# Delta rule on one Trainium2 core: wider spacing of the inverse's stages, later transposes, and the first block's low weight parts in four pieces

## The chip, the cores and the metric

The kernel runs on one core of a Trainium2 chip. The metric is the device time of one execution in microseconds. Before the change three runs gave 2961.45, 2965.48 and 2971.93 us, with a median of 2965.48 us.

## What is computed

A decoder of two layers over 2048 tokens of width 1024, in float32. The first layer is a gated delta rule with 8 heads of 128, the second a forgetting attention. The change lies in the first layer alone, which is, cut to what matters:

```python
def chunk_gated_delta_rule(q, k, v, g, beta):
    ...
    a_mat = jnp.where(strict, jnp.einsum('bhncd,bhnsd->bhncs', kb, kc) * decay, 0.0)
    sol = lax.linalg.triangular_solve(a_mat, rhs, left_side=True, lower=True, unit_diagonal=True)
    u, w = sol[..., :Dv], sol[..., Dv:]
    ...
    # for each chunk in turn
    v_new = u_i - w_i @ S
    o = (q_i * exp(g_i)) @ S + attn_i @ v_new
    S = S * exp(g_last) + k_dec.T @ v_new

def gdn_mixer(h, w_in, ...):
    qkv, z, a, b = split(h @ w_in)
    qkv = silu(causal_depthwise_conv(qkv, conv_w))   # 4 taps
    ...
    o = rms_norm(o, o_norm) * silu(z)
    return o @ w_out
```

## The kernel before

**Projections.** `gdn` works on four blocks of 512 tokens and in each on four groups of two heads. `project` (L272) computes for a group eight products of 1024 x 128 weights with the block: for each head k, q and v, and then z of both. A product has eight steps. A step is `mm3` (L129): three matmuls of 512 columns, since each operand is kept as a high part that TensorE's fast float32 format holds (wh, xh) and the low rest (wl, xl). A group has thus 64 steps, numbered 1 to 64 here.

**Weights.** In the first block (qt 0) `wsplit` (L283) loads a weight, and `split` (L122) makes the high part by a ScalarE copy (L124) and the low part by one GpSimd subtraction of 1024 columns (L125). Both are stored to `w_d` and loaded from there in the other three blocks (L289, L290). In a group there are eight weights, in the first block 32.

**Tails.** After a product of k, q or v its `tail` (L340) makes the convolution: two ScalarE passes (L343, L347), three VectorE multiply-adds (L349), a tanh on ScalarE (L352) and a last VectorE step into `kq` or `th` (L357). What it returns, `rest` (L361), is kept in `pend` and called in the product after next, behind the step kt == 3: four TensorE transposes (L364), squares (L368), kd (L371) or vR (L398) on ScalarE, and for q the norms (a power on GpSimd, L119), the k k^T products (L387) and the matrix At on VectorE (L391). So k, q, v of the first head and k, q, v of the second have their transposes in steps 20, 28, 36, 44, 52 and 60.

**The inverse and the chain.** `finish` (L416) is a generator that works on a group behind its projections. It sends At through DRAM (L426, L429), inverts 32 x 32 blocks by 31 rounds of a multiply and a subtraction on VectorE (L435, L437), sends the result back (L440, L442), transposes blocks of it into Tn (L445), and joins the blocks by two pairs of TensorE products: px (L451) and py (L462, L464), with a copy X1 between them (L455 on ScalarE, L456 on VectorE), then px2 (L475) and py2 (L482). Then come four chunks with the state S in three stages each (A, B, C: L497, L515, L523), and the outputs: two transposes pto (L554), each followed by a product og on VectorE (L556) and a store (L558). px, py, px2, py2, the chunks and pto take turns in two PSUM banks (pool `gcs`, tag `sc`).

**What sets the order.** `weave` (L587) runs a step of the projections and then looks at each open `finish`: a stage that yields W is followed by W main steps, and the next stage is written behind the step after these. With the weights before, px stands at step 44 of the following group, py at 48, px2 at 51, py2 at 53, the first A at 56, and the two pto at steps 31 and 33 of the group after that. The last group's `finish` runs beside the output projection `Wout.run` (L648, 256 such steps); the next part of the kernel (`hprep`, L732) is begun after it. The written order is what a scheduler starts from: it fixes the order on each engine and on each DMA queue from readiness and this priority, so that an instruction can stand earlier than it is written. Each engine then works in its fixed order, and so does the SP queue, which issues all DMAs here.

Of the kernel before, what the change touches and what calls it, by code (L numbers as in the profile page):

```python
# [14 lines left out]
ALU = mybir.AluOpType  # L15
# [7 lines left out]
KT = D // P  # L23
# [14 lines left out]
def f(ap):  # L38
    return ap.bitcast(F32)
# [82 lines left out]
def split(k, hi, lo, src, eng=None):  # L122

    i = k.nc.scalar.copy(hi, src)  # L124
    (eng or k.nc.vector).tensor_tensor(out=lo, in0=src, in1=f(hi), op=ALU.subtract)  # L125
    return i.ins


def mm3(nc, out, ah, al, bh, bl, start, stop):  # L129
    nc.tensor.matmul(out, ah, bh, start=start, stop=False)  # L130
    nc.tensor.matmul(out, ah, bl, start=False, stop=False)  # L131
    nc.tensor.matmul(out, al, bh, start=False, stop=stop)  # L132


def gdn(k, ins, oT_d, chain, proj_, after_proj):

    nc, tc = k.nc, k.tc
# [55 lines left out]
    def keep():  # L193
        ct, wh, wl = kept.pop(0)
        nc.sync.dma_start(w_d[ct, 0], f(wh))
        nc.sync.dma_start(w_d[ct, 1], f(wl))
# [75 lines left out]
    def project(qt, hg, state, tiles):  # L272
# [10 lines left out]
        def wsplit(col, nm):  # L283

            ct = col // P
            wh = p2.tile([P, KT, P], F32R, tag="wh", bufs=4, name=f"wh_{nm}")
            wl = p2.tile([P, KT, P], F32R, tag="wl", bufs=4, name=f"wl_{nm}")
            if qt > 0:
                nc.sync.dma_start(f(wh), w_d[ct, 0])  # L289
                nc.sync.dma_start(f(wl), w_d[ct, 1])  # L290
                return wh, wl
            wr = p2.tile([P, D], F32, tag="x", bufs=4, name=f"wr_{nm}").rearrange("p (t c) -> p t c", c=P)
            nc.sync.dma_start(wr, w_in[:, col:col + P].rearrange("(t p) c -> p t c", p=P))
            split(k, wh, wl, wr, nc.gpsimd)
            kept.append((ct, wh, wl))
            if len(kept) > 2:
                keep()
            return wh, wl

        def proj(col, nm):  # L300
            wh, wl = wsplit(col, nm)
            pp = pm.tile([P, TB], F32, tag="mm", name=f"pp_{nm}")
            for kt in range(KT):
                mm3(nc, pp, wh[:, kt, :], wl[:, kt, :], xh[kt], xl[kt], kt == 0, kt == KT - 1)
                if kt == 3 and len(pend) > 1:
                    pend.pop(0)()
                yield
            return pp

        for hl in range(G):  # L310
# [11 lines left out]
            for i, gg in enumerate((gh, gl)):  # L322
                nc.gpsimd.tensor_tensor(out=rg[:, i], in0=bc(k.tri, CH),
                                        in1=f(gg[:, :, h:h + 1]).to_broadcast([P, CH, P]), op=ALU.mult)
# [10 lines left out]
            for kind in (1, 0, 2):  # L335
                ct = kind * H + h
                nm = f"{q_}_{ct}"
                pp = yield from proj(ct * P, nm)

                def tail(h=h, hl=hl, us=us, kq=kq, vR=vR, kd=kd, E=E, ssn=ssn, rn=rn, vs=vs, kind=kind, ct=ct, nm=nm, pp=pp):  # L340
# [64 lines left out]
        for hl in range(G):  # L405
            h = hg * G + hl
            pp = yield from proj(3 * D + h * P, f"{q_}_z{h}")
            if hl == 0:
                pend.append(lambda: None)
            th = p2.tile([P, TB], F32, tag="th", bufs=3, name=f"thz_{q_}_{h}")  # L410
            nc.scalar.activation(th, pp, AF.Tanh, scale=0.5)
            nc.vector.scalar_tensor_tensor(out=zT[:, hl, :], in0=th, scalar=1.0, in1=pp, op0=ALU.add, op1=ALU.mult)
# [147 lines left out]
    pend = []  # L560
# [17 lines left out]

W_INV, W_PY, W_PX2, W_PY2, W_A, W_B, W_C, W_OUT, W_OUT2 = 42, 3, 2, 1, 2, 1, 2, 9, 1


H_LAG = 3
# [665 lines left out]
```

## Time and profile before

| | |
|---|---|
| median of three runs | 2965.48 us (2961.45 to 2971.93) |
| the profiled execution's own time | 2970.9 us |
| its span, first to last instruction | 2969.2 us |
| TensorE (PE) busy | 2828.0 us, 95% |
| VectorE (DVE) busy | 1747.6 us, 59% |
| ScalarE (ACT) busy | 1338.5 us, 45% |
| GpSimd (POOL) busy | 674.2 us, 23% |
| mean granted TensorE clock | 0.979 |

The first block of the projections runs to about 300 us of the span, blocks two to four to about 1222 us, and the last group's `finish` beside the output projection to about 1345 us. The rest of the span (the output projection, the shared keys and values, the attention) isn't touched.

PE is TensorE, PEld its weight load, DVE VectorE, ACT ScalarE, POOL GpSimd, SPq the queue that issues DMAs. An idle time stands with what released the instruction after it. A clock of 1.00 is the full 2.4 GHz.

### The profile page before, as it was taken

Reading aid. Unit: us, or ns where it says so; the run is one execution under the profiler, and the core shown is the slowest. Engines: PE = TensorE matmul, PEld = TensorE weight load, DVE = VectorE, ACT = ScalarE, POOL = GpSimd, SP = SyncE. Lnnn points to the kernel's source line nnn. Section 1 sums busy time; section 2 is a strip of 40 time slices with the busy share of each in tenths; the row PEclk is TensorE's granted clock in tenths of the full one; section 3 lists DMA queues with packets and bytes.
Section 4 is the critical chain, followed back from the end, with each engine's and each line's share of the span. In section 5 each row is a group of like instructions: output and inputs, shape, how many; then the busy total and the mean of one; then the engine's idle time right before and its main releaser. Section 6 shows DMA issues by size and latency. Waiting matters only on the chain.

```text
span 2969.2 us, 50594 instructions
## 1 busy us (share of the span) xinstructions
PE 2828.0 (95%) x18406; PEld 2450.9 (83%) x18406; DVE 1747.6 (59%) x5053; ACT 1338.5 (45%) x3695; POOL 674.2 (23%) x617
## 2 busy tenths in 40 slices
PE   7889999999999999899999999999999999999998
PEld 5667778777777777777899999999997888888787
DVE  6777767777777776644333223432228888888422
ACT  4445544454445444433344323443216676776421
POOL 4433111111111111022311000111004444443222
PEclk9999999999999999989999999999999999999999
DMA  6555444444443444536322323333222333232443
GB/s 215 180 176 182 163 134 146 134 151 142 135 133 127 140 134 135 155 119 195 110 90 86 96 96 111 98 101 94 96 83 89 93 100 99 91 96 82 145 147 107
DMA packets 295504, 371.63 MB, mean 125 GB/s; under 512 B 68443, under 2 KB 216150, under 8 KB 294230
## 3 DMA queue, kind: packets, MB, share of 16 engines
q1 hardware_dynamic: 295254, 368.39, 38.6%
q8 instruction: 145, 2.38, 0.3%
q14 instruction: 105, 0.86, 0.1%
HBM read 263.40 MB, written 104.92 MB: 124 GB/s over the span
## 4 chain that ended last, share of the span: by engine, by line
PE 59%; DVE 17%; issue 7%; ACT 3%; DMA 3%; POOL 3%; SPq 0%; DVEq 0%; POOLq 0%; ACTq 0%
DVE acc_q L349 4%; PE pt L1075 4%; PE ps L132 2%; PE ppv L130 2%; PE ppq L130 2%; PE ppv L131 2%; PE ppv L132 2%; PE ppq L131 2%; PE ppq L132 2%; PE ppwf L132 2%; PE ppwf L131 2%; PE ppwf L130 2%; PE ps L130 2%; PE ps L131 2%; PE ppk L130 2%
## 5 line engine op out<-in xcount | busy, mean ns | idle before, releaser
L130 PE MATMUL pp_q<-xh_q,wh_q 128*128 128x512 f32 x768 | 330.2, 430 | 2.1 <-ACT wh_q L124 2.1
L132 PE MATMUL pp_q<-xh_q,wl_q 128*128 128x512 f32 x768 | 309.0, 402 | 1.3 <-POOL wl_q L125 1.3
L131 PE MATMUL pp_q<-xl_q,wh_q 128*128 128x512 f32 x768 | 309.9, 404 | 0.0
L349 DVE SCALAR_TENSOR_TENSOR acc_q<-cx_q,cols,acc_q 128x512 f32<-128x512 f32 x288 | 226.2, 786 | 9.5 <-ACT acc_q L347 6.3
L125 DVE TENSOR_TENSOR pl<-pt,ph 128x512 fp32r<-128x512 f32 (+1 forms) x320 | 191.8, 606 | 39.4 <-ACT ph L124 37.4
L124 ACT CAST ph<-pt 128x512 fp32r<-128x512 f32 (+1 forms) x320 | 161.6, 519 | 92.2 <-PE pt L1075 91.7
L1061 ACT ACTIVATE s<-s,nm 128x128 f32<-128x128 f32 (+15 forms) x128 | 154.2, 1205 | 71.9 <-DVE nm L1059 71.9
L132 PEld LDWEIGHTS pp_q<-xh_q,wl_q 128*128 128x128 f32 x768 | 147.9, 193 | 38.2 <-POOL wl_q L125 2.0
L1075 PE MATMUL pt<-ident,s 128*128 128x128 f32 x1088 | 173.8, 274 | 2.6 <-DVE pl L125 2.5
L130 PEld LDWEIGHTS pp_q<-xh_q,wh_q 128*128 128x128 f32 x768 | 148.8, 194 | 29.6 <-ACT wh_q L124 2.2
L131 PEld LDWEIGHTS pp_q<-xl_q,wh_q 128*128 128x128 f32 x768 | 149.1, 194 | 27.2
L352 ACT ACTIVATE th_q<-acc_q 128x512 f32<-128x512 f32 x96 | 60.7, 632 | 243.5 <-DVE acc_q L349 239.5
L1075 PEld LDWEIGHTS pt<-ident,s 128*128 128x128 f32 x1088 | 134.6, 141 | 33.2 <-DVE pl L125 3.6
L130 PE MATMUL ppk<-wh_k,hh 128*128 128x256 f32 x512 | 147.7, 288 | 2.6 <-issue 2.6
L130 PE MATMUL ppq<-wh_q,hh 128*128 128x256 f32 x512 | 146.8, 287 | 0.0
L130 PE MATMUL ppv<-wh_v,hh 128*128 128x256 f32 (+1 forms) x512 | 144.9, 283 | 0.0
L131 PE MATMUL ppk<-wl_k,hh 128*128 128x256 f32 x512 | 144.5, 282 | 0.0
L132 PE MATMUL ppk<-wh_k,hl 128*128 128x256 f32 x512 | 144.3, 282 | 0.0
L130 PE MATMUL ppz<-wh_z,hh 128*128 128x256 f32 x512 | 144.3, 282 | 0.0
L132 PE MATMUL ppv<-wh_v,hl 128*128 128x256 f32 (+1 forms) x512 | 143.9, 281 | 0.0
L131 PE MATMUL ppv<-wl_v,hh 128*128 128x256 f32 (+1 forms) x512 | 143.9, 281 | 0.0
L131 PE MATMUL ppq<-wl_q,hh 128*128 128x256 f32 x512 | 143.7, 281 | 0.0
(479 smaller groups left out, 8606.5 us busy)
## 6 DMA issues: line engine op xcount, KB each, us to landing
wh_q<-w_d SPq DMA_DIRECT2D x72, 512.0 KB, 3.6
wl_q<-w_d SPq DMA_DIRECT2D x72, 512.0 KB, 4.4
wr_q<-in_gdn_w_in_dram SPq DMA_DIRECT2D x24, 512.0 KB, 5.4
w_d<-wh_q SPq DMA_DIRECT2D x24, 512.0 KB, 5.4
w_d<-wl_q SPq DMA_DIRECT2D x24, 512.0 KB, 3.6
wh_q_z<-w_d SPq DMA_DIRECT2D x24, 512.0 KB, 3.5
wl_q_z<-w_d SPq DMA_DIRECT2D x24, 512.0 KB, 4.1
x_q<-in_x_dram SPq DMA_DIRECT2D x16, 512.0 KB, 4.0
```

The source lines that it names most:

```text
L124: i = k.nc.scalar.copy(hi, src)
L125: (eng or k.nc.vector).tensor_tensor(out=lo, in0=src, in1=f(hi), op=ALU.subtract)
L130: nc.tensor.matmul(out, ah, bh, start=start, stop=False)
L131: nc.tensor.matmul(out, ah, bl, start=False, stop=False)
L132: nc.tensor.matmul(out, al, bh, start=False, stop=stop)
L349: nc.vector.scalar_tensor_tensor(out=acc, in0=cx[:, j:j + TB], scalar=cw[j], in1=acc, op0=ALU.mult, op1=ALU.add)
L352: nc.scalar.activation(th, acc, AF.Tanh, scale=0.5)
L1061: e = nc.scalar.activation(s[:, 0:w], s[:, 0:w], AF.Exp, bias=nm, accum_out=ls[:, ii:ii + 1])
L1075: nc.tensor.transpose(out=pt[:, ii * P:(ii + 1) * P], in_=Ps[ii][:, j * P:(j + 1) * P], identity=k.ident)
```

## The change

The spacing of the stages is widened: 45 main steps in place of 42 ahead of px, 5 in place of 3 ahead of py, 4 in place of 2 ahead of px2, 2 in place of 1 ahead of py2. px then stands at step 47, py at 53, px2 at 58, py2 at 61, the first A at 64, and all later stages eight steps later than before, the two pto at steps 39 and 41. `rest` is called behind kt == 6 in place of kt == 3, so that its transposes stand at steps 23, 31, 39, 47, 55 and 63. In the first block the low part of a weight is made by four GpSimd subtractions of 256 columns; the high part is made as before.

```diff
@@ wsplit, in project
-            split(k, wh, wl, wr, nc.gpsimd)
+            nc.scalar.copy(wh, wr)
+            for i in range(0, KT, 2):
+                nc.gpsimd.tensor_tensor(out=wl[:, i:i + 2], in0=wr[:, i:i + 2], in1=f(wh[:, i:i + 2]), op=ALU.subtract)
@@ proj, in project
-                if kt == 3 and len(pend) > 1:
+                if kt == 6 and len(pend) > 1:
                     pend.pop(0)()
@@
-W_INV, W_PY, W_PX2, W_PY2, W_A, W_B, W_C, W_OUT, W_OUT2 = 42, 3, 2, 1, 2, 1, 2, 9, 1
+W_INV, W_PY, W_PX2, W_PY2, W_A, W_B, W_C, W_OUT, W_OUT2 = 45, 5, 4, 2, 2, 1, 2, 9, 1
```

## Rows read from the trace of the kernel before

**Rows 1.** Stretches: us; PE, PEld, DVE, ACT, POOL busy (x); PEclk, DMA share, GB/s.

```profile
45.00:300.00 255.00, 220.06 (x1205) 175.34 (x1203) 196.26 (x480) 120.09 (x343) 101.80 (x57) 0.95 0.58 188
300.00:1222.00 922.00, 883.03 (x5650) 717.75 (x5650) 660.30 (x2177) 420.53 (x1373) 131.73 (x112) 0.98 0.42 137
1222.00:1345.00 123.00, 110.72 (x596) 88.45 (x597) 67.59 (x191) 47.97 (x125) 26.13 (x26) 0.91 0.53 165
```

**Rows 2.** Line L364 on PE, 30 to 300 us: idle until (us, times).

```profile
  DVE kq_q L357: 11.4, 3
  DVE th_q L357: 6.5, 4
```

**Rows 3.** The same line, 300 to 1222 us.

```profile
  DVE kq_q L357: 5.6, 8
  DVE th_q L357: 4.1, 2
```

**Rows 4.** Line L451 on PE, idle until: 30:300, 300:1222, 1222:1345 in turn.

```profile
  DVE Tn L445: 4.9, 2
...
  DVE Tn L445: 10.0, 14
...
  DVE Tn L445: 4.2, 1
```

**Rows 5.** Line L462 on PE, idle until: 30:300, and then 300:1222.

```profile
  ACT X_q0g L455: 2.0, 1
...
  ACT X_q2g L455: 5.3, 4
  ACT X_q3g L455: 4.8, 3
  ACT X_q1g L455: 3.2, 2
```

**Rows 6.** PE in order of time, 817 to 836 us: start, us, what, [idle before].

```profile
817.67 0.60 PE L554 MATMUL pto_q<-ident,vR_q 128*128 128x128 f32 x4
...
826.01 0.39 PE L130 MATMUL pp_q<-xh_q,wh_q 128*128 128x512 f32 x1
...
826.71 0.40 PE L130 MATMUL pp_q<-xh_q,wh_q 128*128 128x512 f32 x1
...
829.79 0.21 PE L451 MATMUL px_q2g<-Tn,At_q2g 32*32 32x32 f32 x2 [0.43 <-DVE Tn L445]
830.63 0.69 PE L451 MATMUL px_q2g<-Tn,At_q2g 32*32 32x32 f32 x30 [0.63 <-DVE Tn L445]
...
835.91 0.24 PE L462 MATMUL py_q2g<-At_q2g,X_q2g 32*32 32x32 f32 x2 [1.60 <-ACT X_q2g L455]
```

**Rows 7.** DVE in order of time, the same group's inverse and output.

```profile
787.50 0.93 DVE L435 TENSOR_TENSOR tmp_q2g<-Ti_q2g,Ai_q2g 128x31 f32<-128x31 f32 x1
...
824.13 0.74 DVE L556 SCALAR_TENSOR_TENSOR og_q<-pto_q,hon,zT_q2g 128x512 f32<-128x512 f32 x1
```

**Rows 8.** The SP queue's issues in order of time, the same group.

```profile
779.96 1.72 SPq L429 DMA_DIRECT2D Ai_q2g<-d_q2g  x4
...
824.90 0.33 SPq L558 DMA_DIRECT2D oT_d<-og_q  x1
825.40 1.88 SPq L442 DMA_DIRECT2D At_q2g<-d_q2g  x4
```

**Rows 9.** Groups of POOL, 30 to 310 us: busy us, mean ns, idle before.

```profile
L125 POOL TENSOR_TENSOR wl_q<-wr_q,wh_q 128x1024 fp32r<-128x1024 f32 x24 | 57.5, 2397 | 111.2 <-ACT wh_q L124 80.0 <-PE pa_q0g L498 20.0 <-ACT sp_e_q L98 11.1
L119 POOL TENSOR_TENSOR rn_q<-ssn_q,mhalf 128x8 f32<-128x8 f32 x7 | 11.5, 1643 | 26.7 <-DVE ssn_q L374 20.2 <-DVE cx_q L342 4.2 <-DMA w_d<-wh_q_z 2.3
L323 POOL TENSOR_TENSOR rg_q<-tri,gl_q 128x512 fp32r<-128x512 f32 x8 | 8.9, 1108 | 0.0
```

**Rows 10.** Line L437 alone, two groups of heads: DVE busy us (x), clock, DMA.

```profile
176.00:258.00 82.00, 11.66 (x31) 0.96 0.59 187
491.00:561.00 70.00, 7.22 (x31) 1.00 0.44 142
```

## The prediction

> **What bounds the kernel now.** I read the table of stretches first. TensorE is busy in 883.03 of the 922 us of the projection blocks two to four and in 220.06 of 255 us of the first block [rows 1]: it is the engine that the stage waits for, so a wait of TensorE is time of the kernel, and time at the lower clock is too. The granted clock has two levels, 2.4 GHz (1.00) and 1.2 GHz (0.50), so (1 - mean) x length is about what the slow time costs: 255 x 0.05 = 12.8 us, 922 x 0.02 = 18.4 us, 123 x 0.09 = 11.1 us [rows 1].
>
> Then I read who ended TensorE's idle time, line by line. It stands in three places: ahead of a head's transposes L364, which wait for VectorE's last step of the tail (L357): 17.9 us in the first block, 9.7 us later [rows 2, 3]; ahead of the inverse's first product px (L451), which waits for VectorE's transposes Tn (L445): 4.9, 10.0 and 4.2 us [rows 4]; ahead of py (L462), which waits for ScalarE's copy X1 (L455): 2.0 us and 5.3 + 4.8 + 3.2 = 13.3 us [rows 5]. That is 62 us of waits, which the edits aim at one by one. Last I read one group in order of time [rows 6 to 8].
>
> One step of the main loop (three matmuls) starts 0.70 us after the one before: 826.01 to 826.71 [rows 6]. All shifts below are counted in it.
>
> **Transposes three steps later** (`kt == 6`): TensorE reaches each L364 three steps, 2.1 us, later, with the same instructions; nothing is added. In blocks two to four eight waits total 5.6 us, 0.7 us each, and go; two total 4.1 us, and as they are unequal I leave 1.0: 8.7 us gained [rows 3]. In the first block three waits total 11.4 us and four 6.5 us [rows 2]; 2.1 us from each of the long ones and the short ones whole I put at 5.5 + 4.8 = 10.3, leaving 7.6. Ends: nothing (VectorE is later by as much), and 27.6 us. What is queued behind: the head's squares, kd and vR copies on ScalarE, the power on GpSimd, At on VectorE, and the eight DMAs that carry At to the inverse (L426, L429, four each) on SP, all 2.1 us later. These are the price, and they decide the next part.
>
> **W_INV 42 to 45.** px comes at side step 47 in place of 44, 2.1 us later, but the At that feeds the inverse is 2.1 us later as well. Whether anything is gained depends on where the inverse's chain waits. Its input was sent for at 779.96 [rows 8], and the first multiply ran at 787.50 with no idle time before it, behind other work in VectorE's order [rows 7]: I read some us of slack there, so the later At is absorbed. At its end the copy back of At (825.40) was issued right after the store of og (824.90), on the in-order SP queue, and that store waited for og, which ended at 824.13 + 0.74 = 824.87 [rows 7, 8]; og moves eight steps away. So I take 7.5 of the 10.0 us, 2.1 of the 4.9 and 2.1 of the 4.2 [rows 4]: 11.7 us. Ends: 0 and 19.1.
>
> **W_PY 3 to 5.** px ended at 830.63 + 0.69 = 831.32, py started at 835.91 after 1.60 us idle: X1 takes 4.6 us [rows 6]. Six steps in place of four cover 4.2 us, so some 0.4 to 0.5 us of each wait stays: of ten waits with 15.3 us [rows 5], 10.3 us are gained; ends 7 (0.8 each left) and 15.3. **W_PX2 2 to 4 and W_PY2 1 to 2**: I know of no wait there and put them at nothing; the main steps between them cover them. Together the four push every later stage of a group eight steps (5.6 us) back: pto at side steps 39 and 41 of the next group, and the end of the last group eight steps into the output projection, whose 256 steps hide it. If they did not, 5.6 us once.
>
> **The low parts in four pieces.** One takes 2.397 us for 1024 columns, 512 columns of another product take 1.108 us [rows 9], so four of 256 should take no more than the one: 0.6 us each. They matter to VectorE: its 31 subtractions L437 cost 11.66 us in a group of the first block and 7.22 us in a later one with the same 31 [rows 10]. I read the 4.4 us as VectorE held up while GpSimd subtracts; a hold of 0.6 us in place of 2.4 lets the chain behind L357 end sooner. Of the 7.6 us left above I take half, 3.8; ends 0 and 7.6. The ScalarE copy is the same as before. The store of wl on SP waits for the last piece, and the loads queued behind it move with that by tenths.
> The Trainium skill speaks against this edit: the GPSIMD Engine Reference, section "Elementwise — side-by-side cycle accounting", lets every instruction there pay a dispatch through two software hops, beside 156 ns for VectorE's one. By it, an estimate from the page's 156 ns, 96 more instructions would cost at least 15 us of GpSimd, and with all of it on the path the sum below would be 42 us in place of 57. The trace does not agree so far: the rows of 512 and 1024 columns show no such fixed part [rows 9].
>
> **Clock.** Waits gone should take slow stretches with them. I take half of the first block's 12.8 (6.4), 60% of 18.4 (11.0) and a quarter of 11.1 (2.8): 20.2 us; ends 0 and 42.
>
> **New waits.** A new order finds something late. I set 0.5 us for each of 16 groups, 8 us: half a px wait, for a store ahead of At on SP or an og ahead of Tn on VectorE.
>
> **Sum:** 8.7 + 10.3 + 3.8 + 11.7 + 10.3 + 20.2 - 8 = 57 us. The profiled execution took 2970.9 us, so 2913.9; the median of the runs, 2965.5, lies 5.4 us under that execution, so the forecast is 2908.5 us.
>
> **Rivals.**
> 1. **px stays late.** The later transposes hand their delay to At, the inverse ends as much later as px does, and only the other gains stand: minus 11.7, minus half of the clock's 20.2, so 57 - 22 = 35 us and 2930. For it: At feeds the inverse directly, and 45 - 42 equals 6 - 3. Against it: the slack at 787.50 [rows 7].
> 2. **Slower: the PSUM bank of og.** px takes the bank of the first pto of the group before (two banks in that pool), which og frees. pto came at 817.67 and og ended at 824.87, 7.2 us later [rows 6, 7]. Now px comes eight steps (5.6 us) behind that pto, before 13 steps. With the same lag px waits 1.6 us in each of 15 groups, 24 us, and the change still gains. It decides from a lag of 5.6 + 57 / 15 = 9.4 us. Where VectorE's order puts og 5.7 us later (as far as from og to px now, 824.13 to 829.79), the wait is 7.3 x 15 = 110 us: 2908.5 + 110 = 3018. For it: og has low priority in that order. Against: the inverse's end and At no longer stand before it once it is eight steps later.
> 3. **The change moves nothing.** Orders on the engines are set by the scheduler from readiness. If it places px and the transposes where they were, 2965. Against: px (829.79) follows the last transposes' step now as the weights in the source say [rows 6].
> 4. **The pieces are dear.** GpSimd's power over 8 columns takes 1.64 us [rows 9]; were a small piece to cost anything like it, GpSimd's 101.80 us of 255 [rows 1] would rise and wl come late. At 15 us lost, 57 - 15 = 42 and 2923. Against: 512 columns at half of 1024. Beside it stands the page's dispatch rule above, which has the same sign.
>
> **How the numbers follow.** Forecast 0.56, rival 1 0.23, rival 2 0.07, rival 3 0.09, rival 4 0.05. The range 2880 to 2952: all ends together would be 9.7 + 17.9 + 19.1 + 15.3 + 42 = 104 us, and I let it reach to 85; at the other end the shift of the transposes alone (19.0 less 8, and little of the clock) gives 13 us, 2952. Outside lie rivals 2 and 3 (0.16) and little more. The forecast's own range is 2885 to 2925. A measurement of this kernel can tell about 0.3%, 8.9 us, from no change: faster is the forecast with rivals 1 and 4, 0.84; same 0.09; slower 0.07.
>
> **What would show it.** In the changed kernel the waits of L364 in blocks two to four are under 1.5 us together, those of L462 under 6 us, those of L451 under 4 us; the mean clock of that stretch is 0.99; L437 in the first block falls below 10 us a group. Wrong if L451 waits as long as before (rival 1), if L451 or L462 is released by og L556 (rival 2), or if the wl pieces sum to over 2.6 us (rival 4).

## The result and the profile after

The changed kernel takes 2920.7 us (median of six runs, 2914.1 to 2933.1) against 2967.4 us for the kernel before: ratio 0.9845, 95% interval 0.9821 to 0.9869, 47 us faster. The profiled execution is the slowest of the six, 2933.14 us with a span of 2931.4. From the pieces on (L296), lines stand two further down than before: L364 is L366, L451 L453, L462 L464, L437 L439, L556 L558.

Stretches first; columns as in [rows 1]. The cuts are at times: the first block ends at 327.2 us here and at 335.7 before, so the first row holds more of its work than in [rows 1].

```profile
45.00:300.00 255.00, 230.62 (x1236) 183.19 (x1234) 180.75 (x492) 119.70 (x347) 127.15 (x144) 0.93 0.61 194
300.00:1180.00 880.00, 855.98 (x5596) 700.23 (x5597) 643.86 (x2158) 414.71 (x1362) 136.85 (x112) 0.99 0.44 142
1180.00:1303.00 123.00, 113.80 (x630) 92.17 (x630) 68.33 (x195) 50.36 (x133) 25.83 (x26) 0.93 0.52 155
```

Where it went, between the first projection matmuls of the groups: the four groups of the first block take 297.4 us (305.7 before), the twelve of blocks two to four 849.9 (883.7), all behind them 1754.2 (1749.9). Of the gain 33.8 us lie in blocks two to four and 8.3 in the first. The stretch behind is hardly touched (only the last group's `finish` runs in it), and its 4.3 us tell nothing: over the fourteen profiles of this document it takes 1737 to 1754 us, with 18 to 50 us at the lower clock level. So a comparison of two profiles is made here in the projections alone.

In the twelve groups of blocks two to four TensorE's idle time falls from 36.9 to 20.1 us and its time at the lower clock level (1.2 GHz) from 37.5 to 6.8 us, of which half is lost: 17 us are waits and 15 are clock (mean 0.98 before, 1.00 now between the blocks' own ends). In the first block idle time falls from 38.7 to 29.2 us, but the time at the lower level rises from 39.0 to 46.1 (mean 0.94 before, 0.92 now).

The waits, line by line. Transposes L366, for 30 to 300 and 300 to 1180 us (against [rows 2, 3]):

```profile
  DVE kq_q L359: 8.9, 5
  DVE th_q L359: 1.2, 1
...
  DVE kq_q L359: 0.7, 2
```

px, L453, for the first block (30 to 327 us), blocks two to four (327 to 1180) and the stretch behind (1180 to 1303), against [rows 4], where no px wait lies between 300 us and the end of the first block:

```profile
  DVE Tn L447: 11.2, 5
...
  DVE Tn L447: 2.9, 7
...
  DVE s1wg L672: 5.2, 1
```

py, L464, for 300 to 1180 us; none in the first block (against [rows 5]):

```profile
  ACT X_q1g L457: 3.3, 4
  ACT X_q2g L457: 1.9, 2
  ACT X_q3g L457: 1.9, 2
  DVE X_q1g L458: 0.9, 4
  DVE X_q2g L458: 0.9, 4
  DVE X_q3g L458: 0.7, 3
  ACT X_q0g L457: 0.4, 1
  DVE X_q0g L458: 0.2, 1
```

L366 fell from 27.6 to 10.8 us and py from 15.3 to 10.2. px did not fall in sum, 19.1 before and 19.3 now, but its waits moved: in blocks two to four they fell from 10.0 to 2.9 us, and in the first block they rose from 4.9 to 11.2. In blocks two to four px also waits for something else than it did. SyncE's issues in a steady group, whose first projection matmul starts at 692.5 us:

```profile
729.63 1.81 SPq L444 DMA_DIRECT2D At_q2g<-d_q2g  x4
...
737.79 0.34 SPq L560 DMA_DIRECT2D oT_d<-og_q  x1
```

The copy back of At now goes out 8 us ahead of og's store, where it went out right behind it [rows 8]. VectorE in the same group, from the last step of the substitution to Tn:

```profile
724.96 0.17 DVE L439 TENSOR_TENSOR Ti_q2g<-Ti_q2g,tmp_q2g 128x8 f32<-128x8 f32 x1
...
727.23 0.17 DVE L540 TENSOR_TENSOR s_q2g<-rq_q2g 128x8 f32<-128x8 f32 x1 [1.75 <-POOL s_q1g L119]
...
727.51 1.66 DVE L554 TENSOR_SCALAR vR_q<-vR_q,s_q1g 128x128 f32<-128x128 f32 x8
...
737.02 0.75 DVE L558 SCALAR_TENSOR_TENSOR og_q<-pto_q,hon,zT_q1g 128x512 f32<-128x512 f32 x1
737.68 0.42 DVE L447 STREAM_TRANSPOSE Tn<-At_q2g 32x256 f32<-32x256 f32 x1
```

The four copies landed 4.1 us after their issue, near 735.5, so Tn has its data and stands behind og in VectorE's order; px waits 0.4 us for it. The lines L540 to L554 are the previous group's normalisation, with its wait for GpSimd's power. In the kernel before they stood elsewhere, inside the substitution of L435 and L437 (same group, from 715.6 us on):

```profile
738.65 0.20 DVE L437 TENSOR_TENSOR Ti_q2g<-Ti_q2g,tmp_q2g 128x42 f32<-128x42 f32 x1
740.46 1.00 DVE L538 TENSOR_TENSOR s_q2g<-rq_q2g 128x8 f32<-128x8 f32 x1 [1.60 <-POOL s_q1g L119]
...
741.46 1.05 DVE L435 TENSOR_TENSOR tmp_q2g<-Ti_q2g,Ai_q2g 128x35 f32<-128x35 f32 x1
742.43 2.06 DVE L552 TENSOR_SCALAR vR_q<-vR_q,s_q1g 128x128 f32<-128x128 f32 x8
744.41 0.18 DVE L437 TENSOR_TENSOR Ti_q2g<-Ti_q2g,tmp_q2g 128x35 f32<-128x35 f32 x1
```

From 738.85 to 744.41, 5.6 us, a single multiply of the substitution gets through.

### The profile page after: what moved, and what is told of

It reads as the page before. It is cut to its first block, busy times and chain, and to the rows that moved or that the text cites. A ratio compares the mean times of both kernels' runs of the same rounds, so it can differ in the third digit from the quotient of the medians.

```text
span 2931.4 us, 50710 instructions
## 1 busy us (share of the span) xinstructions
PE 2814.7 (96%) x18406; PEld 2446.1 (83%) x18406; DVE 1718.0 (59%) x5053; ACT 1334.9 (46%) x3695; POOL 707.4 (24%) x713
## 5 line engine op out<-in xcount | busy, mean ns | idle before, releaser
L125 DVE TENSOR_TENSOR pl<-pt,ph 128x512 fp32r<-128x512 f32 (+1 forms) x320 | 191.8, 605 | 39.5 <-ACT ph L124 37.6
L132 PEld LDWEIGHTS pp_q<-xh_q,wl_q 128*128 128x128 f32 x768 | 146.7, 191 | 34.9 <-POOL wl_q L296 0.4
L132 PE MATMUL ppq<-wh_q,hl 128*128 128x256 f32 x512 | 143.7, 281 | 0.0
```

## Experiments

Twelve kernels; times are medians, ratios against the kernel before on the same chip. "Waits" in an edit are W_INV, W_PY, W_PX2, W_PY2.

**The parts alone.** Edit: `kt == 6` in the kernel before, nothing else.

> Only the transposes are three steps later (kt == 6); spacing and low parts as before. Theory A (each edit ends its own wait): the waits of L364 fall from 27.6 to under 12 us, those of px grow by a little, and the kernel takes some 2945 us. Rival B (the later transposes hand their delay to At and so to the inverse, which needs the 45): the waits of px (L451) grow by 2.1 us in most of the 15 groups, from 19 to over 40 us, and the time stays within 10 us of the kernel before, some 2965 us.

3018.4 us, ratio 1.0188 (1.0168 to 1.0207): 55 us slower. px over the projections:

```profile
  DVE Tn L445: 56.6, 18
  DVE cx_q L342: 4.4, 1
```

The later transposes alone hand their delay on to px: At is late, the substitution begins 5.2 us later and ends 4.3 us later in its group, and px waits 61 us over the projections where it waited 16. The time at the lower clock level in blocks two to four rises with it, from 37.5 to 78.5 us. Rival B has the wait right, but the loss is larger than either theory allowed.

Edit: waits `42, 3, 2, 1` to `45, 5, 4, 2` in the kernel before.

> Only the spacing is wider (45, 5, 4, 2); transposes and low parts as before. Theory A: px waits under 8 us and py waits under 6 us in all, the waits of L364 stay at 25 to 30 us, and the kernel takes some 2940 us. Rival (the stages that come eight steps later wait for the PSUM banks that og frees, or the waits of L364 grow because VectorE has more in front of its tail): L451 or L462 released by L556, or L364 over 35 us, and the time 2955 us or more.

2992.5 us, ratio 1.0110 (1.0091 to 1.0128): 29 us slower. TensorE's largest waits:

```profile
PE pto_q L554 <- DVE vR_q L552: 23.5, 27, 3.9
PE pt_q L364 <- DVE kq_q L357: 19.6, 12, 6.1
PE px_q0g L475 <- DVE Tn L468: 11.8, 3, 7.6
...
```

px waits once over the projections (5.3 us) and py not at all, as hoped; the output's transposes (pto) and px2 do, which neither theory named. py (step 53) now comes behind the transposes of the second head's q (step 52), so on VectorE py's copies stand behind q's rest.

Edit: the four pieces alone, in the kernel before.

> Only the low parts of the first block are made in four pieces. Theory A (VectorE is held up for less time): the waits of L364 in the first block fall from 17.9 us to some 12, and the kernel takes 2957 to 2963 us. Rival C (the pieces are dear: in the changed kernel one took 0.78 to 0.85 us in the mean, in place of 0.6): GpSimd's gain for VectorE is eaten by low parts that come later, and the time is 2967 us or more.

2956.8 us, ratio 0.9978 (0.9968 to 0.9988): 6 us faster.

Edit: the changed kernel with `split(k, wh, wl, wr, nc.gpsimd)` back.

> The changed kernel with the low parts in one piece again. Theory A: 4 to 8 us more than the changed kernel, 2925 to 2929 us, with waits of L364 in the first block some 4 us longer. Rival C (the pieces are dear): the same as the changed kernel or less, 2915 to 2921 us.

2937.1 us, ratio 0.9911 (0.9897 to 0.9925). So the two edits that lose 55 and 29 us alone gain 26 us together, and the pieces add 16 on top of them (20 by the ratios), not 6. The parts cannot be summed.

**Is it order or distance?** Edit: the changed kernel, waits `45, 7, 4, 2`.

> The changed kernel with the py products two steps later (W_PY 7 for 5), so that they come at step 55, the same step as the transposes of the second head's q, and no longer before them. Theory of order (what counts is which of VectorE's two strings of work, the rest of a head's k or q and the inverse's copies, is put first in its queue): the copies of py into At and Tn now stand behind q's rest, as in the kernel with the wider spacing alone, where the px2 products waited 32.8 us for Tn in all; py's own waits (10.2 us in the changed kernel) go, the px2 waits come back at 20 us or more; 2935 to 2955 us against the changed kernel's 2921. Theory of distance (each stage only needs enough steps after the one before it): py's waits go, px2 keeps five steps and does not wait; 2908 to 2916 us.

2959.7 us, ratio 0.9986 (0.9976 to 0.9995): two steps more for py take 39 us back. TensorE's largest waits:

```profile
PE pt_q L366 <- DVE kq_q L359: 26.7, 15, 4.4
PE pto_q L556 <- DVE vR_q L554: 24.1, 30, 2.5
PE px_q0g L477 <- DVE Tn L470: 5.4, 3, 3.7
```

Distance is refuted. Of the order theory the sign and px2's wait for Tn are there, but px2's 11.7 us (all blocks) are little more than half of what it asked for; the larger losses are pto and L366, which it had not named.

Edit: the changed kernel, waits `42, 5, 4, 2`.

> The changed kernel with the inverse's first wait back at 42 steps, so that px comes at step 44, three steps ahead of the second head's k transposes at 47, and py at 49 or 50. Theory of order: px is put ahead of the k transposes, as it was in the kernel with the later transposes alone, where px waited 58 us in all for Tn; here px waits 30 to 60 us and the time is 2945 to 2985 us. Theory of slack in the inverse (the write-back of the diagonal blocks is early enough now, 8.6 us before og's store in the changed kernel, since VectorE is free earlier): px waits under 15 us, and the time is 2915 to 2930 us.

2912.3 us (2909.0 to 2916.4), ratio 0.9826 (0.9810 to 0.9842), not slower than the changed kernel; three of its four runs lie below the fastest of that one's six. px over the projections:

```profile
  DVE Tn L447: 26.4, 14
```

px waits 7 us longer than in the changed kernel (19.3) and py, L464, not at all (10.2 there): what 45 saves at px comes back at py, and nothing is lost without it. The theory that px's place ahead of the k transposes spoils it falls: it has that place here too.

Edit: the changed kernel, transposes back at `kt == 3`, waits `42, 5, 4, 2`.

> The changed kernel with the transposes back at the third step from the start of the projection (kt 3) and the inverse's first wait at 42, so that px comes at step 44 in the same step as the second head's k transposes, and py at 50, still ahead of q's at 52; the wider spacing and the pieces stay. Theory of order: px and py hold their places in VectorE's queue, py and px2 only get more room, so that it lies below the kernel with the pieces alone (2957 us) by about the 10 to 15 us of py's waits: 2940 to 2948 us; what is left to the changed kernel (some 20 to 28 us) is then what the later transposes themselves are worth. Theory that wider spacing hurts by itself (the wider spacing alone took 29 us more): 2965 to 2990 us.

2925.4 us, ratio 0.9870 (0.9856 to 0.9885), better than either theory said. L366 over the projections:

```profile
  DVE kq_q L359: 21.6, 13
  DVE th_q L359: 2.9, 2
```

Against the pieces alone, waits 5, 4, 2 for 3, 2, 1 gain 31 us with the transposes where they were. Against this run, the later transposes (the run before this one) gain 13 us. That is a balance of several waits: L366 waits 18 us less (24.5 to 6.8), py 8 and pto 4 us less, but px 22 us more (3.9 to 26.4), half of that in the first block. So the delay is handed to px here too; the rest only outweighs it. Neither run has W_INV 45.

**What do 5, 4, 2 move?** py, px2 and py2; the chunk steps and normalisation behind them (five steps); and og. Edit: the changed kernel, transposes at `kt == 3`, waits `42, 3, 2, 1`, W_OUT 14 for 9.

> The changed kernel with the transposes back at kt 3 and the inverse's four waits back at 42, 3, 2, 1, while W_OUT goes from 9 to 14: the sum of the waits, and so the step at which a group's output (og) comes, 36 and 38 of the next group's 64, stays that of the run with waits 42, 5, 4, 2 (2925 us); px, py, px2 and py2 come at 44, 48, 51 and 53 as in the kernel before, where og came at 31 and 33. Theory of the output's place (the spacing pays because the previous group's og and its store no longer stand ahead of the write-back of the inverse's diagonal blocks on VectorE and SyncE): most of the gain stays, py's waits of the kernel before (15 us) are given back in part, 2928 to 2942 us, and the write-back lies ahead of og's store. Theory of the stages' own distance (py and px2 need the room): 2950 to 2960 us, as the pieces alone (2957).

2941.8 us, ratio 0.9931 (0.9915 to 0.9948). The place of pto and og alone is worth some 15 of the 31 us; some 16 belong to what moves with py, px2, py2 and the chunk steps. What it does is seen on SyncE: in the kernel before, the copy back of At goes out 38.3 us behind a steady group's first projection matmul, after og's store at 37.8, here at 37.0 with no store ahead of it.

Edit: the same with `kt == 6`.

> The same with the transposes at kt 6: against the run with later transposes alone (3018 us) only the pieces and W_OUT 14 for 9 differ, against the run with waits 42, 5, 4, 2 (2912 us) only where within the group px2 and py2 and the chunk steps stand. Theory of the output's place: the later transposes were bad alone because og, at step 31, came in the very step of a transposition, ahead of the write-back; with og at 36 the waits of px fall from 58 us to under 30 and the time is 2912 to 2935 us. Theory of distance: the later transposes need py and px2 later; 2975 to 3010 us.

2986.0 us, ratio 1.0076 (1.0061 to 1.0091). px over the projections waits 49.7 us. og's place is not what saves the later transposes; the other part is, 2986 - 2912 = 74 us.

So I read the normalisation's place off VectorE's timelines, in us from the first projection matmul of a steady group, with the substitution from the start of its first multiply to the end of its last subtraction:

| kernel | substitution | normalisation | time us |
|---|---|---|---|
| before | 0.4 - 32.9 | 24.9 | 2965 |
| late alone | 5.6 - 37.2 | 25.4 | 3018 |
| W_OUT 14, kt 3 | 0.4 - 32.9 | 24.9 | 2942 |
| W_OUT 14, kt 6 | 5.6 - 37.2 | 25.4 | 2986 |
| waits 42,5,4,2, kt 3 | 5.3 - 30.0 | 34.9 | 2925 |
| waits 42,5,4,2, kt 6 | 5.7 - 31.4 | 34.2 | 2912 |
| changed kernel | 5.6 - 32.6 | 34.7 | 2921 |
| waits alone | 5.4 - 30.7 | 39.5 | 2993 |
| waits 45,7,4,2, kt 6 | 7.7 - 33.2 | 43.0 | 2960 |

With the normalisation inside, the substitution is 32 us long, with it behind, 25 to 27; when it comes later still, pto (some 24 us in all) waits for the scaled vR. In the run with W_OUT 14 and `kt == 6` the chain can be followed to px, in a group that starts at 798.7 us (SyncE, then TensorE):

```profile
835.84 2.53 SPq L442 DMA_DIRECT2D d_q2g<-Ti_q2g  x4
840.24 0.33 SPq L560 DMA_DIRECT2D oT_d<-og_q  x1
840.74 1.87 SPq L444 DMA_DIRECT2D At_q2g<-d_q2g  x4
844.24 0.22 PE L453 MATMUL px_q2g<-Tn,At_q2g 32*32 32x32 f32 x2 [3.47 <-DVE Tn L447]
```

The substitution stands for 5.7 us around the normalisation there and ends 5.8 us later in its group than with the waits 42, 5, 4, 2 (37.2 against 31.4). It is sent to DRAM at its end, and its copy back goes out at 42.1 us in the group against 35.5: later by the 5.8 and by 0.8 more behind og's store, which the delay puts ahead of it again. px then waits 3.47 us for Tn, in the other run 1.44 in the same group. So the trace carries the delay from the normalisation to px; what it costs in time, no run shows by itself. To move it alone, one edit more: `yield 4` ahead of s1, W_OUT 9, otherwise as the run before.

> The run with later transposes, pieces, waits 42, 3, 2, 1 and W_OUT 14 (2986 us) with one thing moved: the previous group's normalisation (s1, its power on GpSimd, the scalings of vR) is issued four steps later, at the step where the run with waits 42, 5, 4, 2 (2912 us) issues it, and W_OUT goes back to 9, so that og stays at steps 36 and 38. In every slow trace so far (before, later transposes alone, pieces alone, W_OUT 14) the normalisation lies inside the 31 steps of the substitution on VectorE, from about 25 to 29 us of a steady group, and in every fast one behind them, from about 34 to 37. Theory of the normalisation's place: it now falls behind the substitution, which ends near 31 us in place of 36.8, the waits of px fall from 50 us to under 30, and the time is 2912 to 2940 us. Theory of the stages' own distance (py and px2 need their five and four steps): the time stays at 2970 us or more wherever the normalisation lies.

2982.3 us, ratio 1.0060 (1.0041 to 1.0079). But VectorE's timeline shows that the edit did not act:

```profile
746.11 1.00 DVE L541 TENSOR_TENSOR s_q2g<-rq_q2g 128x8 f32<-128x8 f32 x1 [1.58 <-POOL s_q1g L119]
...
747.12 1.07 DVE L437 TENSOR_TENSOR tmp_q2g<-Ti_q2g,Ai_q2g 128x54 f32<-128x54 f32 x1
```

The normalisation runs at 25.4 us in the group as before, and the time is the same. I read this as the scheduler's doing, since the source gives it high priority; no run tests that. This run says nothing for or against the theory. What stays open is how much of the 16 and 74 us is the normalisation's place and how much something else that moves with the chunk steps: that it halts the substitution, and that px waits for the substitution's end, is in the traces; what it costs alone is not.

**The pieces.** Edit: the changed kernel, two pieces of 512 columns (`range(0, KT, 4)`).

> The changed kernel with the low part of the first block's weights in two pieces of 512 columns in place of four of 256. If what counts is the time for which one GpSimd instruction holds VectorE's reads of two operands up, about half of the pieces' 16 us is lost: 2926 to 2932 us. If what counts is only that the copy and the difference no longer follow one another as one block, nothing is lost: 2917 to 2923 us. If the piece's own start-up is what costs, fewer pieces are better: 2908 to 2916 us.

2929.0 us, ratio 0.9881 (0.9863 to 0.9898): between one piece (2937) and four (2921), as the theory of the hold has it.

Edit: the changed kernel, waits `42, 5, 4, 2`, eight pieces of 128.

> The changed kernel with the inverse's first wait at 42 (2912 us with four pieces) and the low part of the first block's weights in eight pieces of 128 columns. Theory of the hold (what counts is how long one GpSimd instruction keeps VectorE's two-operand reads waiting): from one piece to two and from two to four the time fell by 8 us each; the next halving gives half of that or less, 2904 to 2911 us. Theory of start-up (each further piece costs GpSimd some 0.1 us, and it has work enough in the first block): 2913 to 2922 us.

2913.9 us, ratio 0.9828 (0.9812 to 0.9844), the same as four (2912.3) and not the further gain that the theory of the hold expected. GpSimd's groups from 30 to 310 us, eight pieces:

```profile
L296 POOL TENSOR_TENSOR wl_q<-wr_q,wh_q 128x128 fp32r<-128x128 f32 x192 | 96.4, 537 | 66.9 <-ACT wh_q L294 56.1 <-ACT sp_e_q L98 10.7
```

Four, in the changed kernel:

```profile
L296 POOL TENSOR_TENSOR wl_q<-wr_q,wh_q 128x256 fp32r<-128x256 f32 x96 | 78.8, 851 | 76.0 <-ACT wh_q L294 59.2 <-ACT sp_e_q L98 11.1 <-DMA w_d<-wh_q 3.3
```

From 537 ns for 128 columns and 2397 for 1024 [rows 9], a column takes (2397 - 537) / 896 = 2.1 ns and an instruction some 0.27 us besides. That is an estimate: the means hold time in which GpSimd itself waits, and the 851 ns for 256 columns lie 50 ns above that line.

What VectorE gets for it is seen in single operations of the run without pieces, GpSimd's product and then VectorE's lines:

```profile
51.19 2.40 POOL L125 TENSOR_TENSOR wl_q<-wr_q,wh_q 128x1024 fp32r<-128x1024 f32 x1 [2.23 <-ACT wh_q L124]
...
51.62 1.99 DVE L344 COPY halo<-cx_q 128x3 f32<-128x3 f32 x1 [0.73 <-ACT cx_q L343]
53.53 2.31 DVE L349 SCALAR_TENSOR_TENSOR acc_q<-cx_q,cols,acc_q 128x512 f32<-128x512 f32 x3
...
45.14 4.36 DVE L349 SCALAR_TENSOR_TENSOR acc_q<-cx_q,cols,acc_q 128x512 f32<-128x512 f32 x3 [0.42 <-ACT acc_q L347]
```

The copy of three columns lasts until 0.02 us behind the product's end (53.61 and 53.59). Three convolution steps take 2.31 us right behind the product, and 4.36 where a product runs beside them from 46.12 to 48.95. The means, 45 to 305 us, one piece (the run without pieces):

```profile
L349 DVE SCALAR_TENSOR_TENSOR acc_q<-cx_q,cols,acc_q 128x512 f32<-128x512 f32 x63 | 67.0, 1064 | 3.0 <-ACT acc_q L347 2.1
...
L344 DVE COPY halo<-cx_q 128x3 f32<-128x3 f32 x20 | 10.3, 515 | 17.7 <-ACT cx_q L343 17.6
```

and four (the changed kernel):

```profile
L351 DVE SCALAR_TENSOR_TENSOR acc_q<-cx_q,cols,acc_q 128x512 f32<-128x512 f32 x68 | 57.7, 848 | 4.4 <-ACT acc_q L349 3.4
...
L346 DVE COPY halo<-cx_q 128x3 f32<-128x3 f32 x22 | 5.7, 257 | 17.0 <-ACT cx_q L345 16.8
```

The same convolution step takes 1064 ns in the mean beside whole products and 848 beside quarters (930 with two pieces; with W_INV 42, 853 with four and 799 with eight), the copy 515 and 257. Single operations do not all follow: in the kernel before, the pieces alone take the copy from 832 to 309 ns and the convolution from 870 to 889, presumably because another order on VectorE puts other operations beside the products. VectorE's busy time over the first block, with the same instructions (552, or 553 with eight), tells it whole: 223.1 us with one piece, 216.3 with two, 207.7 with four; with W_INV 42, 209.5 with four and 197.7 with eight. The Trainium skill's SBUF — State Buffer, section "SBUF: two separate sides", has the two engines share a port pair as an exclusive lock that one instruction holds to its end; the trace agrees, since the held copy ends with the product, and VectorE's busy time falls with each halving of the piece.

The pieces' gain lies in the first block, which takes 311 us without them and 297 with four. TensorE's idle time there falls by 9 us, of which L366 has only 2.7 (13.4 to 10.7), and its time at the lower clock level by 14 (60.1 to 46.1). In the kernel before, the idle time falls by 7 us and the time at the lower level stays (39.0 and 39.7); they are worth less there. Eight pieces free VectorE for 12 us more, but TensorE's idle time only falls from 31 to 28, and its time at the lower level rises by 5.

## Why the prediction was right, and where not

2908.5 us were forecast, 57 us below before; it is 2920.7, 47 us below, inside the forecast's own range (2885 to 2925). As a list of waits the sum holds in part; as a list of prices for edits it does not: of its parts, two lose time alone. That the total comes within 12 us is luck in good part.

- **Transposes, 8.7 + 10.3.** Right as waits: 0.7 us are left in blocks two to four (1.0 said), 10.1 in the first (7.6 said before the pieces, 3.8 with them). As a part it was wrong: alone it costs 55 us, and in its best company it is worth 13.
- **W_INV and px, 11.7.** Wrong in sum: px waits as long as before, and with W_INV 42 the kernel is no slower. In blocks two to four the term came out, 7.1 us gained where 7.5 was said, and W_INV does it (with 42, px waits 11 us there); but the first block loses 6.3 where 2.1 was to be gained, the stretch behind loses 1.0, and without W_INV 45 py would not wait. The block on SyncE did go, as said; Tn is now held by og on VectorE, the thing that the term for new waits named.
- **W_PY and py, 10.3.** Half: 5.1 us. X1 still takes its time, and 0.8 us of a wait is left in the mean (7.5 us, nine waits) where 0.4 to 0.5 was said, with 0.2 us for the half on VectorE beside it.
- **W_PX2 and W_PY2, nothing; eight steps later, hidden.** This is the step that failed. I priced the sum of the waits only by what lies behind it at the end, and not by where it puts the previous group's normalisation and og among the 31 steps of the substitution. That sum decides the sign: with 3, 2, 1 the later transposes lose 55 us, with 5, 4, 2 they gain 13. Of the 31 us that the spacing gains with the early transposes, og's place has some 15 by a run of its own; the normalisation's share is followed in the trace and not priced.
- **Pieces, 3.8.** Sign right, size a fourth of the 16 us beside the other edits; the path was another, since L366 has 2.7 us of it and the rest is other waits and clock. The evidence was a poor one: L437's sums in the three full groups of the first block that I compared are 7.30 + 10.78 + 6.61 = 24.7 us with one piece and 8.69 + 8.99 + 7.90 = 25.6 with four, so nothing was gained there beside the other edits, while in the kernel before the pieces alone take them from 28.3 to 26.0. Which operations the hold falls on changes with the order; VectorE's busy time as a whole shows it. So the sign "L437 below 10 us a group" came true, but the run without pieces has the smaller sum. The line "wrong if the pieces sum to over 2.6 us" was a bad test: four sum to 3.4 us, and it pays. A fixed cost per instruction, for which the prediction names the Trainium skill's GPSIMD Engine Reference, section "Elementwise — side-by-side cycle accounting", is there too (0.27 us by the estimate above), though on GpSimd and not on the path; my counter-evidence, a product of another kind at half the columns, did not show it.
- **Clock, 20.2.** 15 us in blocks two to four (11.0 said) and a loss of 3.6 in the first block (half of 46.1 - 39.0; a gain of 6.4 said); by the rows some 2.5 in the stretch behind (2.8 said).
- **Rivals.** The first, the delay handed to px, is true of the transposes alone, and stronger than it was priced: it costs 55 us, since px's waits bring slow stretches with them (half of 78.5 - 37.5 is 20 us). It also holds in the first block of the changed kernel, where px waits 11.2 us for 4.9. The spacing is what keeps it small behind that. The second was wrong in its mechanism (no wait of px on L558 of note); the time it gave, 3018 us, is that of the later transposes alone by chance. The third and the fourth are refuted.

## What to carry to other kernels

In a software pipeline whose stages are spaced by fixed counts, the sum of the counts is an edit of its own, since it decides which work of the previous round meets which serial chain of this one on an in-order engine: before pricing the parts, write down the steps at which all stages fall, and look which of them waits for another engine (here 1.75 us for GpSimd) with a long chain behind it. Split a long instruction that holds another engine up, and look where it stops paying: here four pieces of 0.85 us, a third of it fixed cost, pay, and eight of 0.54 us pay no more. Measure the held engine's busy time as a whole, not one operation that looks slow.

## What was not expected of the hardware

A VectorE copy of three columns took 1.99 us beside one GpSimd product of 1024 columns (0.17 us without one), and ended 0.02 us behind the product: its time is that of the other engine's instruction.

Of the clock: the first block's mean fell from 0.94 to 0.92, though the same work there (267.1 and 268.2 us of TensorE's busy time) was done in 297 us instead of 306. The profiles, one execution each, say which edits bring it: the time at the lower level in the first block is 39.0 us before, 66.6 with the later transposes alone, 53.6 with the waits alone, 60.1 with both, 39.7 with the pieces alone and 46.1 with all. What in the order does it, no run shows.

The waits `42, 5, 4, 2` with four or eight pieces, 2912 and 2914 us, were the fastest kernels; with the changed kernel's interval (0.9821 to 0.9869) overlapping that with four (0.9810 to 0.9842), they are at best some 8 us ahead of it.
